# Two transformer blocks on one core: the second block's attention weights split ahead of their stage, and its stick-breaking queries scaled in the sigmoid

## Chip, cores and metric

The kernel runs on 1 core of one Trainium2 chip. The metric is device time in microseconds (us), the median of three runs. The arithmetic uses five engines: TensorE (PE) multiplies matrices, VectorE (DVE) and ScalarE (ACT) work element by element, GpSimd (POOL) does a few elementwise sums, and SyncE (SP) issues most of the transfers (DMA). Each has its own queue of instructions and works through it in order.

## What is computed

The input x has 512 tokens of width 1024. The first block is one layer of sliding-window attention and one pooling layer. The second block has two layers, each a mixer (attention) and a feed-forward part. All weights and results are float32. Cut to what matters here:

```python
def second_block(x, w_in, w_o, ...):
    for l in range(DEPTH):                                  # DEPTH = 2
        h = rmsnorm_2(x, attn_norm[l])
        proj = einsum('bsd,de->bse', h, w_in[l])            # 1024 -> 3072
        sb_q, sb_k, sb_v, df_q, df_k, df_v = split(proj, ...)
        sb_out = stick_breaking_attention(sb_q, sb_k, sb_v) # 8 heads of 64
        ...                                                 # rope on df_q, df_k
        df_heads = differential_attention(dq, dk, dvv, lam) # 4 heads, two maps each
        ...                                                 # norm of the heads
        x = x + einsum('bse,ed->bsd', concatenate([sb_out, df_out]), w_o[l])
        h = rmsnorm_2(x, mlp_norm[l])
        u = square(relu(einsum('bsd,df->bsf', h, w_ff1[l])))
        x = x + einsum('bsf,fd->bsd', u, w_ff2[l])
    return rmsnorm_2(x, final_norm)

def stick_breaking_attention(q, k, v):                      # per head
    z = (q @ k.T) * d ** -0.5                               # 1/8
    strict = kpos < qpos
    log_keep = where(strict, log_sigmoid(-z), 0)
    between = reverse_cumsum(log_keep) - log_keep
    w = where(strict, exp(log_sigmoid(z) + between), 0)
    return w @ v
```

## The kernel before

**Matmuls in three products.** PE reads float32 at a rounded precision (type fp32r), so each operand is kept as two parts: hi, the rounded copy, and lo, what is left. A product of a weight W and an activation X is hi x hi, hi x lo and lo x hi, summed in one PSUM bank. A weight tile is 128 rows by 8 x 128 columns (512 KB). `weights` (L374) loads it into a buffer `wst` (two of them), ACT copies it to `whi` (L385) and DVE subtracts to `wlo` (L388); there are three buffers of each. `lin` (L400) multiplies one such tile with the 512 tokens: 24 matmuls of 512 columns for 8 pieces of the inner dimension. `lin_tokens` (L428) makes the values with tokens on the partitions: two weight tiles, 96 matmuls of 256 columns into two banks at once.

**PSUM.** The eight banks are named by use: two `lin`, three `sc`, two `pv`, one `tr`. A bank that holds a projection comes free when its last reader is done; `drained` tells the ordering when that is expected.

**Stages.** Sliding-window attention (`swa_layer`, to about 182 us), the pool stage (`pool_layer`, to 354), mixer 0 (`mixer_layer`, to 602), feed-forward 0 (`ff_layer`, to 954), mixer 1 (to 1202), feed-forward 1 (to the end). In a mixer the loop over i makes K, Q and, for even i, V tiles: i = 0 to 3 for pairs of stick-breaking heads, i = 4 to 7 for the differential heads. The weights are 8 for K, 8 for Q and 8 for V in each mixer, 24 in all, and 16 half tiles of the output projection. Projections of later i are interleaved with the heads of earlier ones: the loop waits for `heads[i - 2]`.

**Stick-breaking queries.** `on_q` (L1203) evacuates the query projection from PSUM with the norm's factor per token and 0.125 in one DVE instruction (`evac`, L698, its scaled form L703), then `both` (L737) makes for each of two heads the hi part twice (ACT, L744 and L745) and the lo part (DVE, L746). In `sb_head`, `scores` adds a mask (L1056), takes the sigmoid on ACT (L1058), 1 - sigmoid (L1061), runs a product scan on DVE (L1064), multiplies (L1065), and `flip` transposes and splits the weights of attention (L1078, L1079). The norm's factor is kept in two shapes: as rows, `nrm.r`, and as a column per block of 128 tokens, `nrm.rc`, which the values already use.

**Order of work.** `Order` writes the instructions down with generators that wait on estimated times. Then the kernel is built twice: `Plan` takes the instructions of the first build with their dependencies, gives each a cost (`cost`, L197; a DVE instruction is its elements by 0.96 per ns plus 69 ns, and a scan has no price of its own), simulates the engines, SP and a DMA queue at 360 bytes per ns, ranks by the latest start, and returns one order for each of PE, ACT, DVE, POOL and SP. The second build follows these orders, and dependencies are kept by semaphores.

**Feed-forward and pool.** `ff_layer` makes 32 projections `ff1` of the first layer: eight, then for each of four groups one of the next group, eight of the second layer, and the seven others of the next group. `pool_layer` has four groups g of two u tiles and two z tiles, with windowed sums on GpSimd (L978), a mixing product, and then eight tiles of the output projection.

Of the kernel before, what the change touches and what calls it, by code (L numbers as in the profile page):

```python
# [20 lines left out]
P = 128  # L21
# [3 lines left out]
KT = 8  # L25
# [80 lines left out]
class Plan:  # L106
# [91 lines left out]
    def cost(self, k, i):  # L198
# [18 lines left out]
        elif e == "DVE":  # L217
            small = sum(1 for x in src[1:] if free(x) == 1) + (len(aps) > 1)
            fast = op in ("TensorCopy", "TensorScalarPtr") and len(src) - small <= 1 and not any(map(psum, src + aps))
            self.dur[k] = n / (1.92 if fast else 0.96) + 69.0 + (61.0 if small else 0.0)  # L220
            self.port[k] = fast or sum(1 for x in src if free(x) > 1 and not psum(x)) > 1
        else:
            self.dur[k] = 147.0 + 2.105 * n
            self.port[k] = op != "Memset"
# [83 lines left out]
def two_blocks_kernel(ctx: ExitStack, tc: tile.TileContext, a, out, log, orders=()):  # L308
# [57 lines left out]
    def fetch(src, nk=KT, first=None):  # L366
# [6 lines left out]
        return st  # L373

    def weights(src, nk=KT):
        with tc.high_priority():
            st = staged.pop(0) if staged else fetch(src, nk)
# [581 lines left out]
    def pool_layer(nrm, nxt):  # L959
        pin = a["pool_in"]  # L960
        pool = open_pool("pool", "u ws pz pe pth ptl tnh og uh ul")
        outs = [Val() for _ in range(8)]
# [42 lines left out]
        for g in range(4):  # L1005
            for t in (2 * g, 2 * g + 1):
                ps = yield from lin(pin[t], nrm.xs)
                on_u(t, ps)
            for t in (2 * g, 2 * g + 1):
                ps = yield from lin(pin[8 + t], nrm.xs)  # L1010
                on_z(t, ps)
# [14 lines left out]
        for k in range(KT):  # L1026
            ps = yield from lin(a["pool_out"][k], outs)
            add_to_x(k, ps)
            nxt(k)
# [3 lines left out]

    def sb_head(KS, QH, QL, vt, p0, O, done):

# [14 lines left out]
        def scores(qt):  # L1050
# [6 lines left out]
            w = sb([P, S], F32, "sbw", 3)  # L1057
            table("share", nc.scalar.activation(w[:, :n], z[:, :n], AF.Sigmoid))  # L1058
            give(sc_banks, 2000.0)
# [117 lines left out]
    def mixer_layer(l, nrm, old, x_done, xd, nxt):  # L1177
        w2 = a["w_in2"][l]
        low[0] = nc.vector
        mix = open_pool(f"mix{l}", "uh ul cs mdf qs pkh pkl v")  # L1180
        inner = []
# [6 lines left out]
        def scale_cs(r):  # L1188
            for j in range(2):
                nc.gpsimd.tensor_mul(cs[:, j, :], cs[:, j, :], r)  # L1190
        after(nrm.r, scale_cs)
        outs = [Val() for _ in range(8)]
        Ks, Qs = ([Val() for _ in range(8)] for _ in range(2))
# [9 lines left out]
        def on_q(i, ps):  # L1203
            def go(r):
                qf = evac(ps, r, 0.125) if i < 4 else roped(ps, cs)
                put(Qs[i], both(qf, lows), 4500.0)
            after(nrm.r, go)

        def sb_pair(i):
# [17 lines left out]
            for h in range(2):  # L1227
                pe.spawn(sb_head(Ks[i].v[h], *Qs[i].v[h], Vs[2 * i + h].v, 64 * h, O, done))

# [15 lines left out]
        for i in range(8):  # L1245
            c = (4, 0) if i < 4 else (12, 8)
            if i >= 2:
                yield heads[i - 2]
            ps = yield from lin(w2[c[0] + i], nrm.xs, "sc" if i == 1 else "lin")
            on_k(i, ps)  # L1250
            ps = yield from lin(w2[c[1] + i], nrm.xs, "sc" if i == 1 else "lin")
            on_q(i, ps)
            if i % 2 == 0:
                ps = yield from lin_tokens(a["v2"][l][i // 2], nrm.xs, "pv" if i == 0 else "lin")
                on_v(nrm, ps, Vs[2 * i:2 * i + 4] if i < 4 else Vs[4 + i:6 + i])
# [28 lines left out]
    def ff_layer(l, nrm, nxt, end=None):  # L1284
        ff = open_pool(f"ff{l}", "uh ul ev2")

# [14 lines left out]
        def ff1(c, j, U):  # L1301
            ps = yield from lin(a["w_ff1"][l][8 * c + j], nrm.xs)
            U.append(Val())
            on_1(U[-1], ps)

        spread[0] = 1
# [279 lines left out]
```

## Time and profile before

| | |
|---|---|
| median of three runs | 1567.04 us (1566.33 to 1567.07) |
| the profiled execution's own time | 1568.69 us |
| its span from first to last instruction | 1566.8 us |
| mean granted TensorE clock | 0.996 |
| busy: PE, weight load, DVE, ACT, POOL | 1531.6, 1276.1, 1114.5, 778.4, 117.6 us |
| moved by DMA | 147.21 MB, mean 94 GB/s |

Busy time of an engine is the time covered by at least one of its instructions. A matmul's bar also covers the time in which it passes through the array, so the bars of neighbours overlap and their sum is more than the busy time. In the rows below a group shows line, engine, operation, what it writes and reads, shapes and count, then busy us, the mean ns of one, and the idle time before it.

### The profile page before, as it was taken

The numbers are of one execution on the slowest core, as the hardware profiler recorded it, in microseconds if no ns is written. First come the engines' busy times: TensorE is split into PE (matmuls) and PEld (weight loads), VectorE is DVE, ScalarE is ACT, GpSimd is POOL, SyncE is SP. The second block draws the span as 40 slices with busy tenths as digits, with TensorE's granted clock in tenths as the row PEclk, the third lists the DMA queues.
The fourth block names the chain that finished last, engine by engine and source line by source line (L and its number), as shares of the span: only waits on it lengthen the run. The fifth ranks groups of instructions, "written<-read, shape, count | busy, mean of one in ns | idle before, by whom it ended". The sixth has DMA issues, their size and how long they took to land.

```text
span 1566.8 us, 20047 instructions
## 1 busy us (share of the span) xinstructions
PE 1531.6 (98%) x7478; PEld 1276.1 (81%) x7478; DVE 1114.5 (71%) x1929; ACT 778.4 (50%) x1387; POOL 117.6 (8%) x125
## 2 busy tenths in 40 slices
PE   9999999999999999999999999999999999999997
PEld 7878888888778878888888888778888888888886
DVE  7899886778999988536354555899998635445454
ACT  6677563356788866222122234778876312222233
POOL 0000002400000000101010101000000201011010
PEclk9999999999999999999999999999999999999998
DMA  5211332334112223222332234212133323323221
GB/s 178 81 63 47 118 125 94 115 101 142 54 55 65 77 82 128 95 94 94 106 95 96 95 128 135 68 49 73 38 104 115 108 94 95 102 95 100 94 94 68
DMA packets 48227, 147.21 MB, mean 94 GB/s; under 512 B 5488, under 2 KB 7680, under 8 KB 48128
## 3 DMA queue, kind: packets, MB, share of 16 engines
q1 hardware_dynamic: 43824, 136.73, 26.6%
q0 software_dynamic: 1632, 5.22, 1.0%
q10 hardware_dynamic: 2672, 3.97, 0.8%
q8 instruction: 59, 0.97, 0.2%
q14 instruction: 40, 0.33, 0.1%
HBM read 139.60 MB, written 6.29 MB: 93 GB/s over the span
## 4 chain that ended last, share of the span: by engine, by line
PE 76%; DVE 15%; ACT 6%; issue 2%; DMA 1%; DVEq 0%; ACTq 0%; POOLq 0%
PE lin L351 43%; PE sc L351 28%; PE pv L351 4%; DVE sbr L1064 3%; DVE sbw L1065 1%; DVE wlo L388 1%; DVE wtl L1079 1%; DVE qs L713 1%; ACT sqt L1105 1%; PE tr L358 1%; ACT whi L385 1%; ACT p L827 1%; DVE ev L701 1%; DVE pkl L746 1%; DVE sc L1056 0%
## 5 line engine op out<-in xcount | busy, mean ns | idle before, releaser
L385 ACT ACTIVATE whi<-wst 128x1024 fp32r<-128x1024 f32 (+1 forms) x268 | 263.0, 983 | 588.7 <-PE lin L351 274.8
L388 DVE TENSOR_TENSOR wlo<-wst,whi 128x1024 fp32r<-128x1024 f32 (+1 forms) x268 | 354.7, 1324 | 42.6 <-ACT whi L385 41.6
L351 PE MATMUL lin<-xh,whi 128*128 128x512 f32 x672 | 266.7, 397 | 1.6 <-DVE whi L382 1.6
L351 PE MATMUL lin<-xh,wlo 128*128 128x512 f32 x672 | 264.3, 393 | 0.5 <-DVE wlo L383 0.5
L351 PE MATMUL lin<-xl,whi 128*128 128x512 f32 x672 | 264.5, 394 | 0.0
L351 PE MATMUL lin<-uh,whi 128*128 128x512 f32 (+1 forms) x480 | 187.7, 391 | 1.5 <-DVE xh L1263 1.5
L351 PE MATMUL lin<-uh,wlo 128*128 128x512 f32 (+1 forms) x480 | 186.8, 389 | 0.0
L351 PE MATMUL lin<-ul,whi 128*128 128x512 f32 (+1 forms) x480 | 185.6, 387 | 0.0
L351 PEld LDWEIGHTS lin<-xh,wlo 128*128 128x128 f32 x672 | 126.5, 188 | 26.3 <-DVE wlo L383 0.9
L351 PEld LDWEIGHTS lin<-xh,whi 128*128 128x128 f32 x672 | 126.5, 188 | 25.5 <-issue 2.3
L351 PEld LDWEIGHTS lin<-xl,whi 128*128 128x128 f32 x672 | 126.6, 188 | 23.9 <-DVE xl L636 0.5
L351 PE MATMUL sc<-xh,whi 128*128 128x512 f32 x368 | 143.9, 391 | 0.1
L351 PE MATMUL sc<-xh,wlo 128*128 128x512 f32 x368 | 143.7, 391 | 0.0
L351 PE MATMUL sc<-xl,whi 128*128 128x512 f32 x368 | 143.3, 389 | 0.0
L1295 POOL TENSOR_TENSOR ev<-ev 128x512 f32<-128x512 f32 x64 | 68.6, 1071 | 658.9 <-DVE ev L1290 658.9
L793 DVE TENSOR_TENSOR xm<-xm,lin 128x512 f32<-128x512 f32 x38 | 26.2, 688 | 115.2 <-PE lin L351 115.2
L351 PEld LDWEIGHTS lin<-uh,wlo 128*128 128x128 f32 x480 | 90.2, 188 | 19.5
L351 PEld LDWEIGHTS lin<-uh,whi 128*128 128x128 f32 x480 | 90.3, 188 | 19.3 <-DVE xh L1263 2.0
L351 PEld LDWEIGHTS lin<-ul,whi 128*128 128x128 f32 x480 | 90.2, 188 | 18.6
L351 PE MATMUL sc<-uh,whi 128*128 128x512 f32 (+1 forms) x232 | 90.3, 389 | 0.0
L351 PE MATMUL sc<-uh,wlo 128*128 128x512 f32 (+1 forms) x232 | 90.0, 388 | 0.0
L351 PE MATMUL sc<-ul,whi 128*128 128x512 f32 (+1 forms) x232 | 89.2, 385 | 0.0
(250 smaller groups left out, 2818.7 us busy)
## 6 DMA issues: line engine op xcount, KB each, us to landing
wst<-in_w_ff_dram SPq DMA_DIRECT2D x128, 512.0 KB, 3.5
wst<-in_w_in_dram SPq DMA_DIRECT2D x32, 512.0 KB, 3.5
wst<-in_attn_in_dram SPq DMA_DIRECT2D x18, 512.0 KB, 3.6
wst<-in_pool_in_dram SPq DMA_DIRECT2D x16, 512.0 KB, 3.5
wst<-in_v_dram SPq DMA_DIRECT2D x16, 512.0 KB, 3.5
wst<-in_w_o_dram SPq DMA_DIRECT2D x32, 256.0 KB, 2.6
wst<-in_attn_out_dram SPq DMA_DIRECT2D x16, 256.0 KB, 2.7
wst<-in_pool_out_dram SPq DMA_DIRECT2D x8, 512.0 KB, 3.5
```

The costliest lines, as they stand in the source:

```text
L351: i = nc.tensor.matmul(o, lhsT=l, rhs=r, start=start, stop=stop, skip_group_check=True)
L358: nc.tensor.transpose(o, i, ident)
L385: c = nc.scalar.activation(hi[:, :nk, :], st[:, :nk, :], AF.Copy)
L388: low[0].tensor_sub(lo[:, :nk, :], st[:, :nk, :], f32(hi[:, :nk, :]))
L701: nc.vector.tensor_mul(t, ps, r)
L713: nc.vector.tensor_sub(t[o0:o0 + 64, :], src[p0:p0 + 64, :], f32(t[p0:p0 + 64, :]))
L746: nc.vector.tensor_sub(lo[p0:p0 + 64, :], s, f32(h[p0:p0 + 64, :]))
L793: nc.vector.tensor_add(x[k], x[k], ps)
L827: nc.scalar.activation(pt[:, j, :w], pt[:, j, :w], AF.Exp, scale=-1.0, bias=negm[:, j:j + 1], accum_out=den[:, j:j + 1])
L1064: nc.vector.tensor_tensor_scan(r[:, 1:n][:, ::-1], back, back, 1.0, op0=ALU.mult, op1=ALU.min)
L1065: nc.vector.tensor_mul(w[:, :n - 1], w[:, :n - 1], r[:, 1:n])
L1295: nc.gpsimd.tensor_mul(t2, t, t)
```

## The change

Thirty-six of the second block's attention weights are split into hi and lo before their stage: every second one of mixer 0's 24 (12: the first layer's Q tiles and second halves of V) in `pool_layer`, one after each u tile and one after each of the first four output tiles, and all 24 of mixer 1 in feed-forward 0, one after each of the first 24 `ff1`. `split_ahead` loads the tile into a buffer of its own, copies and subtracts as `weights` did, and stores both parts in DRAM. In the mixer `weights` then loads the two parts straight into `whi` and `wlo`, with no ACT or DVE instruction. The other 12 weights of mixer 0, the output projections and everything else go as before.

The stick-breaking queries are split straight from PSUM, with no evacuation and no factor; `nrm.rc` x 0.125 is made once as a small tile `rq`, and the sigmoid takes its column as scale. The bank is told to be free 3500 ns later in place of 900.

The planner's cost of a scan on DVE goes from 0.96 to 0.48 elements per ns.

```diff
@@ -217,7 +217,8 @@
         elif e == "DVE":
             small = sum(1 for x in src[1:] if free(x) == 1) + (len(aps) > 1)
             fast = op in ("TensorCopy", "TensorScalarPtr") and len(src) - small <= 1 and not any(map(psum, src + aps))
-            self.dur[k] = n / (1.92 if fast else 0.96) + 69.0 + (61.0 if small else 0.0)
+            scan = "Scan" in type(i).__name__ + op or getattr(i, "is_tensor_tensor_scan", False)
+            self.dur[k] = n / (1.92 if fast else 0.48 if scan else 0.96) + 69.0 + (61.0 if small else 0.0)
             self.port[k] = fast or sum(1 for x in src if free(x) > 1 and not psum(x)) > 1
         else:
             self.dur[k] = 147.0 + 2.105 * n
@@ -372,7 +373,46 @@
             order(d, acts.pop("xdma"))
         return st
 
+    ahead = {}
+
+    def mixer_weights(l):
+
+        w = {}
+        for i in range(8):
+            c = (4, 0) if i < 4 else (12, 8)
+            w["k", l, i] = a["w_in2"][l][c[0] + i]
+            w["q", l, i] = a["w_in2"][l][c[1] + i]
+            if i % 2 == 0:
+                for s in range(2):
+                    w["v", l, i // 2, s] = a["v2"][l][i // 2][s]
+        return w
+
+    def split_ahead(name, src):
+
+        st = sb([P, KT, P], F32, "ast", 2)
+        nc.sync.dma_start(st, src)
+        hi = sb([P, KT, P], F32R, "ahi", 2)
+        nc.scalar.activation(hi, st, AF.Copy)
+        lo = sb([P, KT, P], F32R, "alo", 2)
+        nc.vector.tensor_sub(lo, st, f32(hi))
+        kept = []
+        for t in (hi, lo):
+            ctr[0] += 1
+            d = dpool.tile([P, KT, P], F32, tag=f"wd{ctr[0]}", name=f"wd{ctr[0]}")
+            nc.sync.dma_start(d, f32(t))
+            kept.append(d)
+        ahead[name] = kept
+
+    def weight(w, name):
+        return ahead.get(name, w[name])
+
     def weights(src, nk=KT):
+        if isinstance(src, list):
+            with tc.high_priority():
+                parts = [sb([P, KT, P], F32R, tag, 3) for tag in ("whi", "wlo")]
+                for t, d in zip(parts, src):
+                    nc.sync.dma_start(f32(t), d)
+            return parts
         with tc.high_priority():
             st = staged.pop(0) if staged else fetch(src, nk)
             hi = sb([P, KT, P], F32R, "whi", 3)
@@ -958,7 +998,8 @@
 
     def pool_layer(nrm, nxt):
         pin = a["pool_in"]
-        pool = open_pool("pool", "u ws pz pe pth ptl tnh og uh ul")
+        pool = open_pool("pool", "u ws pz pe pth ptl tnh og uh ul ast ahi alo")
+        todo = list(mixer_weights(0).items())[1::2][:12]
         outs = [Val() for _ in range(8)]
         ps_ = [Val() for _ in range(8)]
         As = [Val() for _ in range(8)]
@@ -1006,6 +1047,8 @@
             for t in (2 * g, 2 * g + 1):
                 ps = yield from lin(pin[t], nrm.xs)
                 on_u(t, ps)
+                if todo:
+                    split_ahead(*todo.pop(0))
             for t in (2 * g, 2 * g + 1):
                 ps = yield from lin(pin[8 + t], nrm.xs)
                 on_z(t, ps)
@@ -1025,13 +1068,15 @@
                 on_mix(2 * g + d, ps)
         for k in range(KT):
             ps = yield from lin(a["pool_out"][k], outs)
+            if todo:
+                split_ahead(*todo.pop(0))
             add_to_x(k, ps)
             nxt(k)
         spread[0] = 0
         close_pool(pool)
 
 
-    def sb_head(KS, QH, QL, vt, p0, O, done):
+    def sb_head(KS, QH, QL, rq, vt, p0, O, done):
 
 
         th = sb([P, PACK], F32R, "wth", 2)
@@ -1055,7 +1100,7 @@
             mm(z[:, :n], QL[:, qt * P:n], KS[:, :n], False, True)
             nc.vector.tensor_add(z[:, n - P:n], z[:, n - P:n], msb)
             w = sb([P, S], F32, "sbw", 3)
-            table("share", nc.scalar.activation(w[:, :n], z[:, :n], AF.Sigmoid))
+            table("share", nc.scalar.activation(w[:, :n], z[:, :n], AF.Sigmoid, scale=rq[:, qt:qt + 1]))
             give(sc_banks, 2000.0)
             left = sb([P, S], F32, "sbl", 2)
             nc.scalar.activation(left[:, :n], w[:, :n], AF.Identity, scale=-1.0, bias=one)
@@ -1175,9 +1220,9 @@
         put(val, split(o, "dh", "dl", 4, [P, S]), 6000.0)
 
     def mixer_layer(l, nrm, old, x_done, xd, nxt):
-        w2 = a["w_in2"][l]
+        w2 = mixer_weights(l)
         low[0] = nc.vector
-        mix = open_pool(f"mix{l}", "uh ul cs mdf qs pkh pkl v")
+        mix = open_pool(f"mix{l}", "uh ul cs mdf qs pkh pkl v rq")
         inner = []
         mdf = sb([P, S], F32, "mdf", 1)
         nc.gpsimd.dma_start(mdf, a["mdf"])
@@ -1189,6 +1234,8 @@
             for j in range(2):
                 nc.gpsimd.tensor_mul(cs[:, j, :], cs[:, j, :], r)
         after(nrm.r, scale_cs)
+        rq = sb([P, 4], F32, "rq", 1)
+        after(nrm.rc, lambda rc: nc.vector.tensor_scalar(rq, rc, 0.125, None, op0=ALU.mult))
         outs = [Val() for _ in range(8)]
         Ks, Qs = ([Val() for _ in range(8)] for _ in range(2))
         Vs = [Val() for _ in range(12)]
@@ -1202,9 +1249,14 @@
 
         def on_q(i, ps):
             def go(r):
-                qf = evac(ps, r, 0.125) if i < 4 else roped(ps, cs)
-                put(Qs[i], both(qf, lows), 4500.0)
-            after(nrm.r, go)
+                put(Qs[i], both(roped(ps, cs), lows), 4500.0)
+
+            if i < 4:
+
+                put(Qs[i], both(ps, lows), 4000.0)
+                drained(ps, 3500.0)
+            else:
+                after(nrm.r, go)
 
         def sb_pair(i):
             for v in (Vs[2 * i], Ks[i], Qs[i]):
@@ -1225,7 +1277,7 @@
                     put(heads[i], None, 0.0)
 
             for h in range(2):
-                pe.spawn(sb_head(Ks[i].v[h], *Qs[i].v[h], Vs[2 * i + h].v, 64 * h, O, done))
+                pe.spawn(sb_head(Ks[i].v[h], *Qs[i].v[h], rq, Vs[2 * i + h].v, 64 * h, O, done))
 
         def df_pair(i):
             for v in (Vs[4 + i], Ks[i], Qs[i]):
@@ -1243,15 +1295,14 @@
             pe.spawn(task())
 
         for i in range(8):
-            c = (4, 0) if i < 4 else (12, 8)
             if i >= 2:
                 yield heads[i - 2]
-            ps = yield from lin(w2[c[0] + i], nrm.xs, "sc" if i == 1 else "lin")
+            ps = yield from lin(weight(w2, ("k", l, i)), nrm.xs, "sc" if i == 1 else "lin")
             on_k(i, ps)
-            ps = yield from lin(w2[c[1] + i], nrm.xs, "sc" if i == 1 else "lin")
+            ps = yield from lin(weight(w2, ("q", l, i)), nrm.xs, "sc" if i == 1 else "lin")
             on_q(i, ps)
             if i % 2 == 0:
-                ps = yield from lin_tokens(a["v2"][l][i // 2], nrm.xs, "pv" if i == 0 else "lin")
+                ps = yield from lin_tokens([weight(w2, ("v", l, i // 2, s)) for s in range(2)], nrm.xs, "pv" if i == 0 else "lin")
                 on_v(nrm, ps, Vs[2 * i:2 * i + 4] if i < 4 else Vs[4 + i:6 + i])
             pe.spawn(sb_pair(i) if i < 4 else df_pair(i))
         low[0] = nc.vector
@@ -1282,7 +1333,8 @@
 
 
     def ff_layer(l, nrm, nxt, end=None):
-        ff = open_pool(f"ff{l}", "uh ul ev2")
+        ff = open_pool(f"ff{l}", "uh ul ev2 ast ahi alo")
+        todo = list(mixer_weights(l + 1).items()) if l + 1 < DEPTH else []
 
         def on_1(u, ps):
             def go(r):
@@ -1302,6 +1354,8 @@
             ps = yield from lin(a["w_ff1"][l][8 * c + j], nrm.xs)
             U.append(Val())
             on_1(U[-1], ps)
+            if todo:
+                split_ahead(*todo.pop(0))
 
         spread[0] = 1
         U = []
```

## Rows read from the trace of the kernel before

**Rows 1.** The page: span, and busy time of the engines in part 1.
```profile
span 1566.8 us, 20047 instructions
PE 1531.6 (98%) x7478; PEld 1276.1 (81%) x7478; DVE 1114.5 (71%) x1929; ACT 778.4 (50%) x1387; POOL 117.6 (8%) x125
```

**Rows 2.** The chain of waits: start, length, what (merged).
```profile
365.81 11.51 PE pv L351 x96
...
609.33 5.44 PE sc L351 x24
```

**Rows 3.** PE in order of time, mixer 0: start, length, operation.
```profile
534.33 0.28 PE L351 MATMUL sc<-qs,pkl 128*128 128x128 f32 x1
534.44 0.28 PE L351 MATMUL sc<-qs,pkh 128*128 128x128 f32 x1
```

**Rows 4.** Busy by stage: stretch, length, engines with counts, clock, DMA share, GB/s.
```profile
core 0: us, PE busy (x) PEld busy (x) DVE busy (x) ACT busy (x) POOL busy (x), PEclk, DMA share, GB/s
60.00:182.00 122.00, 120.86 (x623) 99.66 (x622) 116.23 (x330) 84.97 (x225) 2.15 (x4) 1.00 0.23 73
182.00:353.80 171.80, 171.80 (x759) 142.00 (x758) 131.42 (x189) 77.73 (x109) 31.24 (x32) 1.00 0.33 108
353.80:602.40 248.60, 239.65 (x1341) 203.51 (x1340) 230.96 (x475) 192.20 (x375) 5.73 (x6) 1.00 0.25 81
602.40:953.80 351.40, 351.10 (x1539) 288.65 (x1539) 182.29 (x184) 97.64 (x118) 34.12 (x33) 1.00 0.32 104
953.80:1202.20 248.40, 239.02 (x1340) 203.42 (x1339) 222.59 (x460) 187.90 (x369) 6.52 (x10) 1.00 0.24 77
```

**Rows 5.** Busy time, as rows 4, in the two parts of mixer 0's heads.
```profile
395.00:480.00 85.00, 78.83 (x477) 66.62 (x476) 81.76 (x154) 68.48 (x134) 0.00 (x0) 1.00 0.17 56
480.00:605.00 125.00, 122.22 (x642) 103.03 (x642) 114.81 (x265) 96.73 (x198) 2.19 (x4) 1.00 0.26 85
```

**Rows 6.** The chain of waits within the stick-breaking heads of mixer 0.
```profile
427.07 0.69 DVE wtl L1079
427.76 1.13 DVE sbr L1064
...
429.26 0.61 DVE sbw L1065
```

**Rows 7.** Groups of DVE in mixer 0, by form.
```profile
L388 DVE TENSOR_TENSOR wlo<-wst,whi 128x1024 fp32r<-128x1024 f32 x22 | 26.7, 1219 | 0.8 <-ACT whi L385 0.6
...
L703 DVE SCALAR_TENSOR_TENSOR ev<-lin,rstd 128x512 f32<-128x512 f32 x3 | 2.0, 682 | 0.1
```

**Rows 8.** Groups of ACT in mixer 0, by form.
```profile
L385 ACT ACTIVATE whi<-wst 128x1024 fp32r<-128x1024 f32 x23 | 24.3, 1057 | 7.6 <-PE pv L351 3.9 <-PE sc L351 1.9 <-PE lin L351 1.7
...
L634 ACT ACTIVATE xh<-xm,par 128x512 fp32r<-128x512 f32 x6 | 4.3, 712 | 0.0
...
L626 ACT ACTIVATE sqt<-xm 128x512 f32<-128x512 f32 x5 | 3.1, 626 | 1.3 <-DVE xm L1272 1.3
```

**Rows 9.** The page, part 6: transfers, KB each, median us to landing.
```profile
wst<-in_w_ff_dram SPq DMA_DIRECT2D x128, 512.0 KB, 3.5
...
wst<-in_w_o_dram SPq DMA_DIRECT2D x32, 256.0 KB, 2.6
...
xd<-xm SPq DMA_DIRECT2D x8, 256.0 KB, 2.0
```

**Rows 10.** Groups of DVE and of POOL in the pool stage, by form.
```profile
L388 DVE TENSOR_TENSOR wlo<-wst,whi 128x1024 fp32r<-128x1024 f32 x28 | 38.3, 1366 | 4.7 <-ACT whi L385 4.6
...
L978 POOL TENSOR_TENSOR ws<-ws 128x525 f32<-128x525 f32 x6 | 11.6, 1937 | 0.5
```

**Rows 11.** Busy time, as rows 4: the pool stage's last third; the start.
```profile
300.00:353.80 53.80, 53.80 (x239) 44.54 (x239) 42.14 (x59) 26.46 (x38) 5.50 (x7) 1.00 0.37 123
...
0.00:50.00 50.00, 46.37 (x239) 38.85 (x240) 37.25 (x76) 29.83 (x53) 3.04 (x9) 0.97 0.46 161
```

**Rows 12.** Groups of DVE by line, feed-forward 0.
```profile
L388 DVE TENSOR_TENSOR wlo<-wst,whi 128x1024 fp32r<-128x1024 f32 x65 | 104.5, 1610 | 13.7 <-ACT whi L385 13.7
```

**Rows 13.** Groups of DVE by line, mixer 0.
```profile
L1064 DVE TENSOR_TENSOR_SCAN sbr<-sbl 128x127 f32<-128x127 f32 (+3 forms) x32 | 26.1, 815 | 1.6 <-ACT sbl L1061 1.4
```

## The prediction, made before the change was run

> **What bounds the kernel now.** I read the page first, then where matmuls run back to back, then busy time by stage, the chain of waits inside an attention stage, the groups by line of VectorE (DVE) and ScalarE (ACT), and last the transfers. The page shows PE busy for 1531.6 of 1566.8 us, which would leave 35 us to win anywhere [rows 1]. That share flatters, since in the profile a matmul's bar is longer than its step. What a matmul costs is read where they run back to back: 24 of 512 columns take 5.44 us, so 0.2267 each, and 96 of 256 columns take 11.51 us, so 0.12 each [rows 2]; two of 128 columns start 0.11 us apart [rows 3], and I put 384 columns between, at 0.173.
>
> By these steps the stages differ. In the pool stage and in the first feed-forward stage (ff) PE runs almost without a hole [rows 4]. One attention (mixer) stage, counted from the code, has 648 matmuls of 512 columns (16 projections of 24, the output projection's 192, 72 in the heads and norms), 444 of 256, 60 of 384 and 180 of 128 (120 of them transposes), 1332 where the row counts 1341. That is 146.9 + 53.3 + 10.4 + 19.8 = 230.4 us of PE, against stages of 248.6 and 248.4 us [rows 4]. So **each mixer stage loses 18 us**. In the first mixer PE stands idle for 6.2 us in 395 to 480 (stick-breaking heads) and 2.8 us in 480 to 605 (differential heads) [rows 5]; I divide the 18 us alike, 12 and 6. The second mixer repeats this.
>
> What takes them is DVE. It is busy 81.8 of 85 us in the first part and 114.8 of 125 in the second [rows 5], and the chain there goes from one DVE instruction to the next, subtraction, scan, product, for heads and weights in turn [rows 6]. ACT has 16.5 us free in those 85. In the pool stage DVE is busy 131.4 of 171.8 us and in ff 182.3 of 351.4 [rows 4]: there is room there.
>
> **The change part by part.** *Weights split ahead.* Today each 128x1024 weight costs one DVE subtraction of 1219 ns [rows 7] and one ACT copy of 1057 ns [rows 8] in the mixer. Twelve of the first mixer's 24 and all 24 of the second's move out: DVE loses 14.6 and 29.3 us there, ACT 12.7 and 25.4. In their place each weight is two transfers of 512 KB into the same buffers of three. Such a transfer lands 3.5 us after its issue [rows 9]; a buffer freed is needed two weights (10.9 us of PE) later, so both halves fit, and I put this at nothing. On the SP queue each load waits until PE has let go of its buffer; behind it stand the loads of the next weights, which wait for the same, so it holds up nothing else. Were that cover gone, PE would wait for the second half, 1.5 us per weight (524 KB at the 350 GB/s worked out below).
>
> *The same work in the pool stage and ff.* A subtraction beside GpSimd's work takes 1366 ns in the pool stage [rows 10]: 12 make 16.4 us, and DVE has 40 free. In its last third DVE is already at 42.1 of 53.8 us [rows 11]; the four splits in the output projection (5.5 us) leave it 6. In ff it is 24 times at most 1.61 us [rows 12], 39 us where 169 are free, and ACT has 254 free for 25. What can go wrong is order: an engine that has begun a split is held for 1 to 1.6 us, and GpSimd's window sums (up to 1937 ns each [rows 10]), which feed the pool projections, come after DVE's evacuation. Bounds: nothing, or 1.4 us for each of the 36, 50 us. PE runs without a hole in the pool stage now beside 28 such subtractions [rows 10], so it is near the low end: I take 1 us for each stage, 2 together.
>
> *Stick-breaking queries.* The evacuation with the factor 0.125 (682 ns of DVE, 4 in a mixer [rows 7]) goes: 2.7 us. Two subtractions and four copies then read PSUM in place of SBUF; I price that at no change, since the evacuation itself shows 0.68 us for 512 elements from PSUM. The sigmoid gets its factor from a column: ACT with such an operand takes 712 ns where without it takes 626 [rows 8], so 32 x 0.09 = 3 us of ACT per mixer. What is late next is the bank: it was free after one DVE instruction, and now waits for four copies and two subtractions, at least 4 x 0.6 + 0.7 = 3 us. Behind it on PE stands the projection after next; at the third pair the values need both banks at once. Bounds: nothing (heads fill PE), or 4 x 3 us a mixer. I take 1 us a mixer, for that one pair.
>
> *The planner's price of a scan.* Only the order changes. The 32 scans take 26.1 us of DVE in a mixer [rows 13]; by the old price, n/0.96 + 69 ns, they were 12.8. The order was made for a DVE with 13 us more than it has, in the very part where PE idles. Bounds: a loss of a few us from a new order, or much of the 18 us; I take nothing for it alone.
>
> **The sum.** In the first part of the second mixer DVE falls from 81.8 by 8 x 1.22 and three evacuations to 70.0 us, below PE's 73 (85 - 12). DVE at 95% of the time is what the sliding-window stage has (116.2 of 122), and PE idles 1.1 of 122 us there [rows 4] against 6.2 of 85 here. I take a loss of 4%, so 76 us, a gain of 9. In the second part (119 us of PE) DVE falls to about 105: 2.5 us of the 6 stay lost, a gain of 3.5. In the first mixer, with half the weights gone, DVE still needs 74.9 us in the first part, above PE's 73: at its present 96% that takes 78, a gain of 7. In the second part it falls to 110: a gain of 2. That is 12.5 + 9 = 21.5 us, less 2 for pool and ff and 2 for the banks: **17 us**. The profiled execution took 1568.7 us (span 1566.8), 1.7 above the median of the three runs; 1568.7 - 17 = 1551.7, or **1550 us** on the median's scale.
>
> **The rivals.** *A, the relief goes unused.* ACT (96.7 of 125 us in the second part [rows 5]) and the longer bank take DVE's place. For it speaks that ACT gets 3 us of sigmoid; against it that ACT loses 10 and 22 us net. Then some half of the 21 is gained, 10 us, less 3: 1560.
>
> *B, more than the sum.* The truer price lets the planner fill PE, and the mixers come within 1.5 us each of their 230.4. For it: 13 us of DVE that it did not see; against: even the sliding-window stage is not free of idle time. It gives 1567 - 33 + 4 = 1538.
>
> *C, slower: transfers in ff.* While first-layer weights are projected, each 5.44 us would carry the weight, the split weight's load and two stores: 4 x 0.524 MB, 385 GB/s. The rows bear 350 GB/s at full share (161 at 0.46 [rows 11]). The first eight then need 48 us for 43.5 of PE, 4.4 us behind, and so twice more, since 24 splits go over three bursts of eight. It decides once the lag passes the four weights fetched ahead (22 us), or a fetch stands on the SP queue behind a store that waits for its subtraction. Then 13 us are lost, and with as long a wait on the queue 26; with 20 between, 1567 - 17 + 20 = 1570. Against it: transfers use 0.32 of the engines in ff now [rows 4], a store of 256 KB lands in 2.0 us where a load takes 2.6 [rows 9], and eight weights of the second layer, with no split, follow each burst.
> The Trainium skill (DMA: Bandwidth & Descriptors, section Specifications) limits a core to about 358 GB/s at HBM, which speaks against the change; by it the lag is 3.4 us a burst. Its page HBM Reference (section Specifications) lets a core that streams alone have some 425 GB/s, and by that there is none. The row's 350, which I go by, is nearer to the first; no run here has asked for as much yet.
>
> **How the numbers follow.** The forecast holds 0.62 (1542 to 1557), A 0.16, B 0.10, C 0.07; 0.05 is left for a change within 0.2%, 3 us, which is about what a measurement here can tell. The range 1538 to 1562 takes in the forecast, A and B and leaves out C and no change. Faster: 0.62 + 0.16 + 0.10 = 0.88; same 0.05; slower 0.07.
>
> **What would show it.** Right: in both mixers the idle time of PE falls, most in the part that begins 41 us after the stage's start; the second mixer is shorter than the first by some 3 us; DVE is busy near 191 us in it and near 214 in the first; pool and ff last as long as before; transfers rise by 36 x 4 x 0.524 = 75 MB. Wrong: ff longer, with waits for landing weights, or SP waiting for splits (C); ACT the engine that PE waits for in the mixers (A); both mixers alike although one has half the relief, which would say that the order and not the load was the cause (B). The step I trust least is how much of a microsecond freed on DVE comes back on PE.

## The result, and the profile after

The changed kernel takes **1557.48 us** (median of 4, 1557.12 to 1558.95) against 1566.68 us for the kernel before in the same measurement: ratio 0.9944, 95% interval 0.9932 to 0.9956. It is 9.2 us faster. The forecast was 17 faster, 1550 in a range of 1538 to 1562. The measured time lies in that range, half a microsecond above the forecast's own band of 1542 to 1557 and nearer to rival A's 1560 than to 1550.

The page of the kernel after, span and part 1, to be held against [rows 1]:
```profile
span 1555.9 us, 20342 instructions
...
PE 1530.1 (98%) x7478; PEld 1273.7 (82%) x7478; DVE 1097.3 (71%) x1923; ACT 782.9 (50%) x1387; POOL 127.0 (8%) x125
...
DMA packets 68964, 222.73 MB, mean 143 GB/s; under 512 B 7792, under 2 KB 9984, under 8 KB 68864
```
PE's busy time hardly moved, so what went is idle time. Where, the busy time by stage of the kernel after shows (the pool stage, mixer 0, ff 0, mixer 1, then the two parts of mixer 0's heads; columns as in [rows 4]):
```profile
180.00:351.10 171.10, 171.10 (x755) 141.44 (x754) 140.99 (x199) 87.38 (x117) 33.41 (x32) 1.00 0.62 221
351.10:596.80 245.70, 240.68 (x1341) 202.89 (x1341) 216.70 (x461) 183.71 (x364) 5.72 (x6) 1.00 0.31 106
596.80:947.70 350.90, 350.87 (x1539) 288.68 (x1538) 195.79 (x205) 119.54 (x139) 42.55 (x33) 1.00 0.59 213
947.70:1191.50 243.80, 238.75 (x1339) 203.19 (x1338) 195.44 (x435) 169.13 (x347) 6.47 (x10) 1.00 0.36 129
...
392.10:477.10 85.00, 81.75 (x506) 70.78 (x505) 77.31 (x149) 67.70 (x131) 0.00 (x0) 1.00 0.27 94
477.10:596.80 119.70, 117.92 (x600) 96.26 (x599) 106.05 (x254) 89.58 (x188) 2.19 (x4) 1.00 0.28 93
```
Mixer 0 went from 248.6 to 245.7 us, mixer 1 from 248.4 to 243.8: 2.9 and 4.6 won. DVE came down in them from 231.0 to 216.7 and from 222.6 to 195.4. The pool stage (171.8 before) and ff (351.4) are a little shorter, not longer, though their DMA share rose from 0.33 to 0.62 and from 0.32 to 0.59. In the first part of the heads PE's idle time fell from 6.2 to 3.3 us [rows 5].

The two profiled spans differ by 10.9 us, more than the medians: 2.0 us of that lie ahead of the pool stage (180.0 us from the span's start, 182.0 before), where the code is the same and the profiled execution of before had a clock drop (last section).

The transfers of the kernel after, the page's part 6 (KB each, median us to landing):
```profile
wst<-in_w_ff_dram SPq DMA_DIRECT2D x128, 512.0 KB, 3.5
wd<-ahi SPq DMA_DIRECT2D x36, 512.0 KB, 6.7
...
whi<-wd SPq DMA_DIRECT2D x36, 512.0 KB, 3.5
wlo<-wd SPq DMA_DIRECT2D x36, 512.0 KB, 4.1
```
The split parts arrive nearly as fast as a raw weight (3.5 and 4.1 against 3.5 us), and no wait for one of them is among the waits below. The stores are slow, but PE never waits for them; DVE does three times, 2.2 us in all.

(Ahead of the prediction three line numbers are wrong: in the kernel before `weights` stands at L375, `lin` at L407 and `cost` at L198. The twelve weights are mixer 0's eight Q tiles and the second tile of each of its four V.)

### The profile page after: what moved, and what is told of

Read it like the earlier page. It is cut to its first block, busy times and chain, and to the rows that moved or that the text cites. A ratio compares the mean times of both kernels' runs of the same rounds, so it can differ in the third digit from the quotient of the medians.

```text
span 1555.9 us, 20342 instructions
## 1 busy us (share of the span) xinstructions
PE 1530.1 (98%) x7478; PEld 1273.7 (82%) x7478; DVE 1097.3 (71%) x1923; ACT 782.9 (50%) x1387; POOL 127.0 (8%) x125
## 4 chain that ended last, share of the span: by engine, by line
PE 81%; DVE 9%; ACT 8%; issue 1%; DMA 1%; ACTq 0%; DVEq 0%; SPq 0%; POOLq 0%
PE lin L352 45%; PE sc L352 30%; PE pv L352 4%; ACT sqt L1150 2%; DVE sbr L1109 1%; PE tr L359 1%; ACT dp L1176 1%; ACT p L867 1%; DVE sbw L1110 1%; DVE wtl L1124 1%; PE sc L359 1%; ACT whi L425 1%; DVE ev L741 1%; PE tr L352 1%; ACT sbw L1103 0%
## 5 line engine op out<-in xcount | busy, mean ns | idle before, releaser
L425 ACT ACTIVATE whi<-wst 128x1024 fp32r<-128x1024 f32 (+1 forms) x232 | 224.2, 969 | 473.1 <-PE lin L352 208.2
L428 DVE TENSOR_TENSOR wlo<-wst,whi 128x1024 fp32r<-128x1024 f32 (+1 forms) x232 | 300.3, 1296 | 31.2 <-ACT whi L425 30.6
L352 PEld LDWEIGHTS lin<-xl,whi 128*128 128x128 f32 x672 | 126.3, 188 | 24.8 <-DVE xl L676 0.5
L1347 POOL TENSOR_TENSOR ev<-ev 128x512 f32<-128x512 f32 x64 | 75.9, 1186 | 653.3 <-DVE ev L1342 653.3
```

The costliest lines, as they stand in the source:

```text
L352: i = nc.tensor.matmul(o, lhsT=l, rhs=r, start=start, stop=stop, skip_group_check=True)
L425: c = nc.scalar.activation(hi[:, :nk, :], st[:, :nk, :], AF.Copy)
L428: low[0].tensor_sub(lo[:, :nk, :], st[:, :nk, :], f32(hi[:, :nk, :]))
L1347: nc.gpsimd.tensor_mul(t2, t, t)
```

## The experiments

The theory was that the load on DVE holds PE up, and that taking it away lets PE run. The rival was that the order does it. The change has three parts (weights, queries, the price of a scan), so the first four runs take them one by one and two together. Each ratio is to the kernel before, run beside it (1566.25, 1566.95 and 1566.36 us in the three groups of runs).

**The scan's price alone**, on the kernel before.
```diff
-            self.dur[k] = n / (1.92 if fast else 0.96) + 69.0 + (61.0 if small else 0.0)
+            scan = "Scan" in type(i).__name__ + op or getattr(i, "is_tensor_tensor_scan", False)
+            self.dur[k] = n / (1.92 if fast else 0.48 if scan else 0.96) + 69.0 + (61.0 if small else 0.0)
```


> The kernel before with the planner's new price of a scan alone. Load theory (the gain is the DVE work that left the mixers): 1566.7 us within 1.5, since no engine has less to do. Order theory (the truer price lets the planner fill PE's holes): 1560 us or less, with less PE idle time in both mixers alike.

Measured: 1560.60, ratio 0.9966 (0.9953 to 0.9978). One number in the planner, with the same work on every engine, gives 5.7 us. Busy by stage, both mixers:
```profile
351.80:597.90 246.10, 240.00 (x1342) 203.90 (x1342) 229.94 (x476) 192.77 (x375) 5.73 (x6) 1.00 0.25 82
948.80:1194.90 246.10, 239.94 (x1339) 203.10 (x1338) 221.38 (x460) 187.51 (x369) 6.47 (x10) 1.00 0.24 78
```
DVE is as busy as before, and yet PE's idle time (length less PE) fell from 9.0 and 9.4 to 6.1 and 6.2.

**The weights alone**: the kernel before with `split_ahead`, old price, old queries.
```diff
+                if todo:
+                    split_ahead(*todo.pop(0))
...
-            ps = yield from lin(w2[c[0] + i], nrm.xs, "sc" if i == 1 else "lin")
+            ps = yield from lin(weight(w2, ("k", l, i)), nrm.xs, "sc" if i == 1 else "lin")
```


> The kernel before with the 36 weights split ahead, with neither the query edit nor the new price. Load theory: most of the gain, 1559 to 1561 us, and mixer 1 (24 weights) shortened by about twice as much as mixer 0 (12). Order theory: 1565 us or more, since the order still rests on scans priced at half.

Measured: 1565.74, ratio 0.9997 (0.9989 to 1.0006): nothing. Busy by stage, both mixers:
```profile
352.40:600.60 248.20, 240.06 (x1342) 203.15 (x1341) 218.24 (x464) 181.63 (x364) 5.73 (x6) 1.00 0.31 104
952.00:1200.10 248.10, 240.73 (x1340) 202.91 (x1340) 197.79 (x438) 168.52 (x347) 6.51 (x10) 1.00 0.36 126
```
The load did leave: DVE is 12.7 and 24.8 us less busy than before. The stages are as long as they were. What PE waited for most in this kernel, in mixer 0 and in mixer 1 (waiter, then who ended the wait: us in total, times, longest):
```profile
PE sc L358 <- DVE sbw L1109: 3.7, 4, 1.7
...
PE sc L358 <- DVE sbw L1109: 1.6, 5, 0.4
```
The same two views of the kernel before, then mixer 1 of the kernel with the scan's price alone, and mixer 0 of the changed kernel:
```profile
PE sc L358 <- DVE sbw L1065: 2.8, 5, 1.1
...
PE sc L358 <- DVE sbw L1065: 4.2, 7, 1.1
```
```profile
PE sc L359 <- DVE sbw L1066: 0.4, 1, 0.4
```
```profile
PE pv L352 <- ACT wth L1123: 1.1, 2, 0.7
PE sc L359 <- DVE sbw L1110: 0.7, 2, 0.4
```
With 12 weights gone, PE waits longer for the product behind the scan than before; with 24 gone it waits less, 1.6 against 4.2 us, but that stage is no shorter either. There PE's idle time fell by 2.0 us and its busy time rose by 1.7 for the same matmuls; why was not separated. With the scan's price alone this wait is down to 0.4 us in mixer 1 and not listed in mixer 0. The planner puts a matmul where it believes that product to be ready, and by the old price a scan of 511 elements takes 0.6 us, where [rows 6] has 1.13.

**The queries alone**, on the kernel before.
```diff
-                qf = evac(ps, r, 0.125) if i < 4 else roped(ps, cs)
-                put(Qs[i], both(qf, lows), 4500.0)
-            after(nrm.r, go)
+                put(Qs[i], both(roped(ps, cs), lows), 4500.0)
+            if i < 4:
+                put(Qs[i], both(ps, lows), 4000.0)
+                drained(ps, 3500.0)
+            else:
+                after(nrm.r, go)
...
-            table("share", nc.scalar.activation(w[:, :n], z[:, :n], AF.Sigmoid))
+            table("share", nc.scalar.activation(w[:, :n], z[:, :n], AF.Sigmoid, scale=rq[:, qt:qt + 1]))
```


> The kernel before with the stick-breaking queries split from PSUM and the factor in the sigmoid, nothing else. Load theory: 4 x 0.68 us of DVE less and 3 us of ACT more per mixer, 1565 us within 1.5. Bank theory (the bank held for six instructions costs PE more than the evacuation did): 1568 us or more. Order theory: 1566.7, no part of the gain.

Measured: 1568.26, ratio 1.0012 (1.0003 to 1.0021): 2 us slower, although it removes DVE work.

**Weights and price without the queries**: the last diff undone in the changed kernel.
```diff
-                put(Qs[i], both(roped(ps, cs), lows), 4500.0)
-            if i < 4:
-                put(Qs[i], both(ps, lows), 4000.0)
-                drained(ps, 3500.0)
-            else:
-                after(nrm.r, go)
+                qf = evac(ps, r, 0.125) if i < 4 else roped(ps, cs)
+                put(Qs[i], both(qf, lows), 4500.0)
+            after(nrm.r, go)
```


> The changed kernel with the query edit undone. Load theory: 1559 us, 1 to 2 above the changed kernel. Bank theory: 1555 us, faster than the changed kernel. Order theory: as the changed kernel, 1557.5.

Measured: 1554.44, ratio 0.9924 (0.9911 to 0.9936), 3 us faster than the changed kernel. So the weights bring 0.5 us under the old price and 6.2 (1560.60 - 1554.44) under the new. Busy by stage, both mixers:
```profile
351.70:594.00 242.30, 238.49 (x1341) 202.88 (x1340) 218.69 (x464) 181.43 (x364) 5.73 (x6) 1.00 0.31 107
945.90:1188.60 242.70, 237.49 (x1340) 203.24 (x1339) 197.68 (x438) 167.66 (x347) 6.46 (x10) 1.00 0.37 129
```
Both mixers are alike to 0.4 us although the second has twice the relief. The prediction named this as the sign that the order is the cause. (In the changed kernel the second is 1.9 us shorter; that difference came with the queries.)

**Is it the right price, or only another order?** The last kernel with 0.72 and with 0.32 elements per ns.
```diff
-            self.dur[k] = n / (1.92 if fast else 0.48 if scan else 0.96) + 69.0 + (61.0 if small else 0.0)
+            self.dur[k] = n / (1.92 if fast else 0.72 if scan else 0.96) + 69.0 + (61.0 if small else 0.0)
```


> The kernel with 36 weights split ahead and the old queries, scans priced at 0.72 elements per ns in place of 0.48. Price theory (the order is good as far as the planner's price is the measured one): between the 1565.7 us of the old price and the 1554.4 of the new, 1557 to 1563. Luck theory (any new order has a time of its own, some 5 us up or down): no such order, anywhere from 1552 to 1568.

> The same kernel with scans priced too high, 0.32 elements per ns. Price theory: not better than 1554.4 us, 1554 to 1560, since DVE is planned with 13 us of work that it does not have. Rival (what helped is only that scans are planned with more slack): 1550 us or less. Luck theory: anywhere from 1550 to 1566.

Measured: 1562.75 (0.9973, 0.9962 to 0.9983) at 0.72, 1558.70 (0.9948, 0.9934 to 0.9961) at 0.32. With 0.96 (the weights alone) that is 1565.7, 1562.8, 1554.4, 1558.7 for 0.96, 0.72, 0.48, 0.32: the time is least at the price that the trace bears out (511 elements by 0.48 and 69 ns are 1.13 us), and worse on both sides.

At 0.32 part of the 4.3 us is the clock: PE waits 3.07 us there for an instruction behind a scan, until 477.99, the granted clock is 0.55 from 476 to 480 and 0.59 from 480 to 484, and the five executions have 0.994 to 0.996 in the mean, against 0.997 and 0.998.

A merely lucky order gives no reason for such a row. Nor does a new order alone move the time so far. In the traces of the next run and of the one that is only told of a longer hold, PE has another kind of matmul at some 720 and 200 of 7478 places than in the kernel at 0.48, and the times differ from it by 0.6 and 0.1 us; at the price 0.72 it is some 820 places and 8.3 us.

**The sigmoid's column alone**: a scale taken from a column of ones.
```diff
-            table("share", nc.scalar.activation(w[:, :n], z[:, :n], AF.Sigmoid))
+            table("share", nc.scalar.activation(w[:, :n], z[:, :n], AF.Sigmoid, scale=one))
```


> The kernel with 36 weights split ahead, the old queries and the new price, and the sigmoid given a column of ones as scale: 90 ns more of ACT for each of 64 sigmoids, nothing else of the query edit. Bank theory (the query edit costs by the PSUM bank that it holds): 1554.4 us within 1. Sigmoid theory (it costs by the longer sigmoid on ACT): 1557 us.

Measured: 1555.03, ratio 0.9922 (0.9909 to 0.9934), 0.6 us over the kernel without the column. The longer sigmoid is not what the queries cost.

**Another price that is wrong.** Where instructions follow each other without a hole, the step from start to start is what one costs. ACT in order of time, mixer 0 of the kernel after (start, us, operation):
```profile
409.53 0.37 ACT L1123 ACTIVATE wth<-sc 128x256 fp32r<-128x256 f32 x1
409.79 0.61 ACT L1106 ACTIVATE sbl<-sbw,one 128x384 f32<-128x384 f32 x1
...
411.02 0.73 ACT L1106 ACTIVATE sbl<-sbw,one 128x512 f32<-128x512 f32 x1
411.78 0.60 ACT L784 ACTIVATE pkh<-lin 64x512 fp32r<-64x512 f32 x1
412.39 0.60 ACT L785 ACTIVATE pkh<-lin 64x512 fp32r<-64x512 f32 x1
```
DVE in order of time, same stage:
```profile
417.90 0.69 DVE L786 TENSOR_TENSOR pkl<-lin,pkh 64x512 fp32r<-64x512 f32 x1
418.63 1.22 DVE L1109 TENSOR_TENSOR_SCAN sbr<-sbl 128x511 f32<-128x511 f32 x1
419.88 0.69 DVE L1141 TENSOR_TENSOR o<-pv,ssa 64x512 f32<-64x512 f32 x1
...
422.59 0.67 DVE L1141 TENSOR_TENSOR o<-pv,ssa 64x512 f32<-64x512 f32 x1
423.19 0.67 DVE L1124 TENSOR_TENSOR wtl<-sc,wth 128x512 fp32r<-128x512 f32 x1
423.79 0.67 DVE L649 TENSOR_TENSOR ul<-o,uh 128x512 fp32r<-128x512 f32 x1
```
Mostly an ACT instruction on 128 partitions is still in its bar when the next one begins (409.53: 0.37 us of bar, a step of 0.26); not so the one at 411.02, which steps 0.76 in front of a copy on 64 partitions. The copy on 64 partitions steps its whole bar, 0.61, where the planner says 0.478. On DVE most instructions on 64 partitions step 0.73 (417.90 to 418.63) where those on 128 step 0.60 (423.19 to 423.79). Not all: the one at 422.59 steps 0.60. Over mixer 0, of instructions of 511 or 512 elements with another right behind them and scans left out, 22 of 31 on 64 partitions step 0.69 to 0.8 on DVE, against 16 of 127 on 128.

The number of partitions is not the whole reason. All 15 subtractions `qs`, which by the program read one half of the partitions and write the other, step at least their whole bar (14 of 16 in the fastest kernel); of the 19 that stay in one half (`pkl`, `o`) 11 do, and the other 8 step 0.60 to 0.61. And of the instructions on 128 partitions 8 of the 10 in front of one on 64 step theirs, of the others about one in ten. So it seems to matter which half is touched; no run tried that apart, and a price by the number of partitions only stands in for it.

So the planner was told, in the kernel with weights and scan price:
```diff
             self.dur[k] = 1300.0 if not aps else n / 1.2 + ...
+            if aps and list(aps[0].ap)[0][1] < P:
+                self.dur[k] += 120.0
 ...
+            if aps and 1 < list(aps[0].ap)[0][1] < P:
+                self.dur[k] += 110.0
             self.port[k] = fast or sum(...)
```


> The kernel with 36 weights split ahead, the old queries and the new price of a scan, and also instructions on fewer than 128 partitions priced as the trace shows their steps, 120 ns more on ACT and 110 ns on DVE (some 80 on ACT and 50 on DVE in a mixer, 14 us). Price theory: faster again, 1549 to 1553 us. Luck theory: no gain to be expected, 1554 within 5. Load theory: 1554.4, no engine has less to do.

Measured: **1540.14, ratio 0.9828 (0.9814 to 0.9841)**, the fastest of all: 14.3 us under the kernel with the same instructions (1554.44), and 17.3 under the changed one. It is 9 us below the least time that was expected of it. No wrong value of this price was tried; three kernels with and without it are faster with it, by 14.3, 5.9 and 8.9 us (the two others follow). Busy by stage, both mixers:
```profile
348.70:585.20 236.50, 235.25 (x1342) 204.14 (x1341) 217.64 (x463) 181.49 (x364) 5.73 (x6) 1.00 0.33 110
936.10:1172.90 236.80, 235.27 (x1340) 203.90 (x1339) 198.29 (x438) 167.95 (x347) 6.49 (x10) 1.00 0.39 132
```
PE idles 1.3 and 1.5 us in them. DVE is within 1.1 us as busy as in the kernel whose mixers took 242.3 and 242.7.

**The two prices without the change**: the kernel before with both, weights split in the mixer, old queries. The edit is the first and the last diff together.

> The kernel before (no weight split ahead, old queries) with both truer prices, of scans and of instructions on fewer than 128 partitions. If the order alone was what PE waited for: 1546 us, the 14 us of the second price off the 1560.6 of the first, and some 6 above the same with weights split ahead. If DVE's load binds once the order is right: 1554 us or more, so that the split ahead is worth 14 us and not 6.

Measured: 1554.71 (1552.34 to 1557.46), ratio 0.9930 (0.9916 to 0.9943). Two prices alone win 11.7 us, at least about as much as the whole change (the intervals of the two ratios overlap). Under them the 36 weights are worth 1554.71 - 1540.14 = 14.6, which is what was expected if DVE's load binds once the order is right. Busy by stage, both mixers:
```profile
348.60:591.00 242.40, 237.40 (x1341) 204.45 (x1340) 229.39 (x475) 191.43 (x375) 5.73 (x6) 1.00 0.26 83
942.10:1185.10 243.00, 238.20 (x1340) 205.53 (x1340) 221.06 (x460) 187.16 (x369) 6.52 (x10) 0.99 0.25 79
```
The weights shorten these mixers by 5.9 and 6.2 us: again alike, though 11.8 and 22.8 us of DVE left, so what left mixer 1 beyond mixer 0's half gave nothing that shows. Part of the 14.6 us is the clock: this kernel's executions had 0.993 to 0.996 in the mean, the slowest the lowest, those of the fastest kernel 0.997 and 0.998.

**The changed kernel with the price for few partitions**, so that the queries stand in an order made with true prices.

> The changed kernel with the second price as well. Bank theory: 1543 us, 3 above the 1540.1 of the same with the old queries. If the 3 us were only an order made with wrong prices of the copies on 64 partitions: 1540 us within 1.

Measured: 1548.58, ratio 0.9885 (0.9872 to 0.9899). Busy by stage, both mixers:
```profile
349.70:592.30 242.60, 237.76 (x1341) 204.15 (x1340) 215.42 (x460) 182.42 (x364) 4.72 (x6) 1.00 0.32 107
943.30:1182.00 238.70, 235.99 (x1339) 203.95 (x1338) 197.28 (x435) 168.56 (x347) 6.46 (x10) 1.00 0.38 131
```
Here the queries cost 8.4 us, 6.1 in mixer 0 and 1.9 in mixer 1, more than either expectation: in each better ordered kernel they have cost more (2.0, 3.0, 8.4). What PE waited for in mixer 0 is led by waits for ACT and one for an evacuation:
```profile
PE pv L356 <- ACT wth L1127: 1.4, 2, 1.0
PE sc L356 <- ACT sbw L1107: 1.3, 1, 1.3
PE lin L356 <- DVE ev L745: 0.7, 1, 0.7
```

**Only told that the bank is held longer**: weights and scan price, old queries, and the estimate of the query bank's release raised from 900 to 3500 ns as in the change.
```diff
-    def evac(ps, r, scale=None):
+    def evac(ps, r, scale=None, lat=900.0):
...
-        drained(ps)
+        drained(ps, lat)
...
-                qf = evac(ps, r, 0.125) if i < 4 else roped(ps, cs)
+                qf = evac(ps, r, 0.125, 3500.0) if i < 4 else roped(ps, cs)
```


> The kernel with 36 weights split ahead, the new price of a scan and the old queries, where only the estimate of when the query's bank comes free is that of the query edit, 3500 ns in place of 900; the instructions are the same. If the query edit costs by the hold itself: 1554.4 us within 1. If it costs by the order that the estimate makes: 1557 us.

Measured: 1554.53, ratio 0.9923 (0.9911 to 0.9936), the same as without. The estimate is not what costs.

**All 24 weights of mixer 0 ahead**, on the fastest kernel: two after each u tile, one after each output tile.
```diff
-        todo = list(mixer_weights(0).items())[1::2][:12]
+        todo = list(mixer_weights(0).items())
...
-                if todo:
+                for _ in range(2):
                     split_ahead(*todo.pop(0))
```


> As the 1540.1 us kernel, with all 24 weights of mixer 0 split ahead in the pool stage, two after each u tile and one after each output tile, 48 in all. Load theory: mixer 0 as short as it can be, 1537 us, with the pool stage unchanged. Rival (the pool stage has no room for 24 subtractions of 1.4 us and the transfers): 1542 us or more, with PE waiting in the pool stage.

Measured: 1548.07, ratio 0.9881 (0.9868 to 0.9895), 7.9 us slower than with twelve. Busy time: mixer 0, the end of the pool stage, the mixer's first 8 us, and 4 us of its heads:
```profile
351.60:592.90 241.30, 237.63 (x1341) 205.29 (x1340) 208.00 (x455) 172.46 (x356) 4.72 (x6) 0.99 0.41 146
...
300.00:351.00 51.00, 49.06 (x217) 40.26 (x216) 43.46 (x62) 28.64 (x39) 1.63 (x3) 1.00 0.91 338
...
352.00:360.00 8.00, 8.00 (x35) 6.04 (x33) 7.61 (x12) 5.62 (x8) 0.00 (x0) 1.00 1.03 420
...
384.00:388.00 4.00, 3.18 (x11) 2.62 (x12) 2.64 (x9) 2.54 (x8) 0.00 (x0) 0.76 0.93 369
```
DVE has 9.6 us less in mixer 0 than in the fastest kernel, and the mixer is 4.8 us longer. PE now idles 1.9 us in the pool stage's last third, and waits 2.33 us for a sigmoid until 384.8, behind which the granted clock drops. What made that sigmoid late is ACT's order. ACT there in order of time:
```profile
381.41 1.28 ACT L756 ACTIVATE qs<-ev 64x512 fp32r<-64x512 f32 x2 [7.01 <-DVE ev L745]
...
383.19 1.28 ACT L1107 ACT_TABLE_LOAD   x1
```
ACT stood idle for 7.01 us, since two copies `qs`, whose input came late, were planned ahead of the load of the sigmoid's table; in the fastest kernel the table is loaded first, at 374.92, and the sigmoid runs before the copies. The chain of waits from 372 to 386 holds no transfer. In the pool stage it does:
```profile
295.13 6.21 DMA ast<-in_w_in_dram
...
302.95 7.29 DMA wst<-in_pool_out_dram
```
A weight to be split lands, ACT copies it, SP issues the store of the copy, and only behind that store the fetch of a weight for the pool stage. ACT's next copy waits for that weight, and PE for what ACT does behind it.

## Why the prediction was right, and where not

**Pool and ff: right, and cheaper.** 2 us were put down; both stages kept their length, PE idling 0.00 and 0.03 us. The transfers rose by 75.5 MB, 75 forecast.

**DVE's load: nearly right.** 214 and 191 us forecast, 216.7 and 195.4 measured.

**That a microsecond off DVE comes back on PE: wrong.** "DVE at 95% of the time" was taken as the bound, and the gains of 9 and 12.5 us hang on it. The weights alone removed 12.7 and 24.8 us of DVE and won half a microsecond, within the noise. PE, DVE and ACT each follow a written order. PE waits for one instruction, which stands where the planner put it, and an engine with more air in an order made for wrong costs gave nothing back. The scan's price alone emptied the wait behind the scan with all the load in place. The fastest kernel's DVE is as busy as that of a kernel 14 us slower. The load is not nothing, though: the same weights won 0.5 us under the old prices, 6.2 with the scan's price and 14.6 with both. So the rule holds in part, in an order made with truer prices: 14.6 us of time for the 34.5 that DVE lost in the two mixers.

**"I take nothing for it alone": the step that failed.** The scan's price was taken at nothing between a loss of a few us and much of the 18; it brings 5.7 alone, and without it the weights bring 0.5. The other planner's price, unknown to the prediction, is worth as much again. Rival B had the larger part of the mechanism (order ahead of load), with the sign that the prediction named for it, both mixers alike where the queries are as before. Its size, 1538, is reached only by the fastest kernel, 1540, not by the change.

**The 18 us a mixer: over-sized.** 248.6 less a floor of 230.4 was taken as loss, but only 9.0 and 9.4 of it was PE idle in [rows 4]. The fastest kernel idles 1.3 us in 236.5 and is still 6.1 over that floor. So some 12 were to be won here, not 18. The other 4.9 us lie within PE's bars, in steps longer than the floor counts, which takes each kind of matmul at its step in a long run: 2.6 us of them in steps next to a change of width, 2.3 spread over all other steps.

**The queries: wrong in sign.** Bank 1 us a mixer, sigmoid hidden, 2.7 us of DVE gained per mixer: together a small gain. They cost 2 to 3 us, and 8.4 with both prices. Not the sigmoid's column (0.6), not the estimate (0.1). What is left is the evacuation's absence: a bank held by six instructions, and splits that read PSUM. That is by elimination only; the hold and the reads were not tried apart, and which of them costs stays open. Rival A is half true here, for ACT leads what PE waits for, though ACT has less work than before.

**Rival C did not come.** It feared full transfers in ff's first burst, at 350 GB/s. Busy time there, kernel after:
```profile
602.40:653.00 50.60, 50.60 (x224) 41.84 (x223) 39.59 (x43) 26.47 (x32) 14.86 (x9) 1.00 0.99 379
```
The engines are full (0.99) for 50 us, and PE has no hole: the price was 350, the chip gave 379. The kernel before had already shown more than 350, 398 GB/s in 4 us of its start (last section); the prediction's row was a mean over 50 us. The Trainium skill's limit for a core at HBM (DMA: Bandwidth & Descriptors, Specifications), 358, is passed by the 379. What the Trainium skill gives for a core that streams alone (HBM Reference, Specifications), some 425, is not passed, with 420 over 8 us as the most here. The rival's second condition, a fetch behind a store on the SP queue, did come in the kernel with all 24 weights of mixer 0 ahead, in the pool stage: 1.9 us.

So the result lies in the range by luck, because terms offset one another. Taken one after the other they are 5.7 us for the price, 6.2 for the weights under it and 3.0 lost by the queries, 8.9 of the 9.2; forecast were 21.5 for the load (a little of it the queries'), nothing for the price, and 4 lost on pool, ff and banks.

## What to carry to other kernels

Before taking load off an engine in a planned order, compare each of the planner's prices with the step from start to start in the trace: here two wrong ones were worth 11.7 us, until the first was right the removed load was worth nothing, and with both right it was worth the most. Busy share does not say whom another engine waits for; what PE waited for, and its idle time by stage, does. Work and traffic that a stage can hide were free when fetched ahead, even at a full transfer share, but not when they were packed still closer before the stage that needs them, where a fetch came to stand behind a store in one queue.

## What the hardware showed that was not expected

Transfers ran at 379 GB/s for 50 us (above), and at 420 over 8 us.

Instructions on 64 partitions mostly do not overlap with their successor: 0.73 against 0.60 us on DVE, 0.61 for an ACT copy from PSUM that the planner had at 0.478. On DVE those that read one half of the partitions and write the other never did (15 of 15 in mixer 0), of the others 8 of 19 did.

The clock fell behind some of PE's long waits, not behind all of them. The start of the profiled execution of before:
```profile
10.00:14.00 4.00, 3.89 (x10) 2.39 (x10) 3.96 (x6) 3.58 (x6) 0.00 (x0) 0.60 1.06 398
```
and in order of time, PE there:
```profile
8.54 0.47 PE L351 MATMUL lin<-xh,whi 128*128 128x512 f32 x1 [1.58 <-DVE whi L382]
...
13.02 0.63 PE L351 MATMUL lin<-xh,wlo 128*128 128x512 f32 x1
13.45 0.63 PE L351 MATMUL lin<-xh,whi 128*128 128x512 f32 x1
```
Behind 1.58 us of idle time the steps go to 0.43, 1.2 GHz, where the kernel after, with 0.83 us of idle time there, has 0.23 at a clock of 1.00. The first loads landed later in that execution. The same followed the wait of 2.33 us in the kernel with all 24 weights ahead and the one of 3.07 us at the scan price 0.32. In the kernel before with both prices PE waits 1.84 us once in each mixer: in the 4 us around the end of the one in mixer 1 the clock is 0.68, around that in mixer 0 it stays at 1.00.
